# Later norm steps in TensorE's order, first FFN subtractions on VectorE, gated casts of weight sums, and w2's last units by halves, in a two-layer hybrid decoder

## The chip, the cores and the metric

The kernel runs on one core of a Trainium2 chip. The metric is device time in microseconds (us). TensorE is called PE below (its weight loads PEld), VectorE DVE, ScalarE ACT, GpSimd POOL, and SyncE SP. Each engine works through its own queue of instructions in order; an instruction waits until what it depends on has signalled.

## The reference

Two post-norm decoder layers over 528 tokens (16 meta tokens and 512 of the input), width 1024, FFN width 2816, all in float32. Cut to what matters:

```python
def hybrid_layer(h, ...):
    proj = jnp.einsum('bld,de->ble', h, w_in)
...
    mix = jnp.einsum('ble,ed->bld', mix, w_out)
    h = layer_norm(ALPHA * h + mix, ln1_g, ln1_b)
    a = jnp.einsum('bld,df->blf', h, w1)
    b = jnp.einsum('bld,df->blf', h, w3)
    y = jnp.einsum('blf,fd->bld', jax.nn.silu(a) * b, w2)
    return layer_norm(ALPHA * h + y, ln2_g, ln2_b)

def layer_norm(x, g, b):
    mu = jnp.mean(xf, axis=-1, keepdims=True)
    var = jnp.mean(jnp.square(xf - mu), axis=-1, keepdims=True)
    y = (xf - mu) * lax.rsqrt(var + LN_EPS)
    return (y * g + b).astype(x.dtype)
```

## The kernel before

**Layout.** Activations lie transposed: 128 of the 1024 channels on the partitions, the tokens along the row, so a full activation is eight tiles. The tokens are worked in two halves, A of 272 and B of 256 (A has 256 in the second layer's mixing and FFN, where the meta tokens are not needed any more). Every product is made of three matmuls on numbers split into a high and a low part: high by high, high by low, low by high (`mm3`, L237 to L239). So one output tile of a half (a unit) is 8 x 3 = 24 matmuls for a sum over 1024 channels, and 33 for one half of w2's 22 blocks.

**Weights** come in chunks of up to 1024 columns. `fetch` (L160) issues the chunk's DMA on SP into one of three `raw` buffers; `ensure` (L173) casts the high part on ACT (L183) and subtracts to get the low part (`sub_lo`, L140) on the engine that the chunk's entry names, DVE or POOL; there are four split buffers `w`. In the FFN the first three hidden blocks (`HEAD = 3`) go the plain way, the rest through a scheme of seven products with sums of weights and of activations (`fast`, L1069); for those, `sums_of` (L190) makes the sums of weights, tag S: a chunk's parts come by SP and by accumulating DMAs that POOL issues (L196, L197), ACT casts (L205, L208, L211, L214), DVE adds and subtracts. A gate (`tc.issue_after(marks["apply", e].ins)`) keeps those ACT and DVE instructions behind the latest marked instruction on their engine.

**The norms.** There are six, named by place and half: m0A and m0B behind layer 0's mixing, f0A and f0B behind its FFN, m1A and m1B behind layer 1's mixing. Each takes eight output tiles as they come: `evac` (L331) adds one to the residual, squares it (ACT L340, the last on DVE L338) and adds it to a running sum (L336) and a running sum of squares (L344), on DVE or POOL by a table; the last of these is `marks["sums"]`. Then three steps on PE. `stats(0)` transposes the sum in three or two blocks (L358), DVE reduces them (L359), and a matmul with ones (L362) spreads the mean. `stats(1)` transposes the sum of squares (L358), DVE reduces (L359) and forms the variance (L365 to L367), POOL takes the power -1/2 (L368), DVE puts it on a diagonal (L371). `apply` spreads that by a matmul (L375); DVE subtracts and multiplies each tile (L380, L381), ACT applies gain and bias (L311) and casts the high part (L313), POOL subtracts the low part (`xl`, L140). These `xh` and `xl` feed the next product. In the first layer POOL and DVE also rotate the retention's queries and keys (L581 to L590), with a DMA in between.

**The order of the work.** PE's instructions are written out by a planner (`Plan`, L60): a piece of work becomes due at the end of the pieces it depends on plus a lag from the table `LAG`, and pieces are issued in the order in which they become due by the planner's own clock. In LAG, `y`, `y2` and `st` are the lags before `stats(0)`, `stats(1)` and `apply`, with a suffix for the norm; `rs_1` is that of the retention output's state product in layer 1 (`ret_out`, L813, L819). A larger lag puts the step behind more of the other matmuls. The other engines' order is made by a scheduler from the same program.

**The FFN's first blocks** (`ffn_hidden`, L1155): three hidden blocks are made the plain way, w1's and w3's product each. ACT takes the silu of the w1 product (L1163). Meanwhile DVE and ACT make the sums of activations (`factors`, L1025: sums L1036 to L1040, high part Th by ACT L1042, low part Tl by DVE). The subtraction of chunks 0 to 3 goes to POOL where `CFG["n0"]` to `CFG["n3"]` is 1, otherwise to DVE; n2 and n3 are 1. On DVE these are placed behind `marks["sums"]`.

**w2 in layer 0** (`ffn_mid`, L1171): its 22 input blocks go in two rounds of 11. A unit's weights are two chunks, 1024 and 384 columns. In the second round units 0 to 5 run for A and B, unit 6 for A, 7 for A and B, then 6 for B from weights loaded again (L1218 to L1230).

Of the kernel before, what the change touches and what calls it, by code (L numbers as in the profile page):

```python
# [12 lines left out]
AF = mybir.ActivationFunctionType  # L13
# [16 lines left out]
EPS = 1e-5  # L30
# [2 lines left out]
N_IN = 21  # L33
PV_L = 40

LAG = dict(T=16.0, g2=3.0, y2=2.0, q=1.5, kb=4.25, fb=3.21, q_1=1.5, kb_1=5.0, fb_1=3.45, rot=8.62, vt=2.86, kt=3.84, kv=1.23, kvo=2.5, rs=2.5, ro=6.35, rp=0.69, f=12.8, a=5.62, b=0.77, v0=9.72, k=3.2, s=0.99, p=2.78, pt=1.24, mt=2.77, u=5.1, rm=3.74, pm=3.74, mx=3.25, y=0.8, st=2.25, ap=2.42, g=2.1, ga=8.46, gn=6.42, gt=21.89, gs=0.33, gs2=0.86, gl=2.0, w=10.8, rot_1=10.43, vt_1=1.2, kt_1=6.88, kv_1=0.74, kvo_1=1.6, rs_1=2.81, ro_1=7.28, rp_1=0.48, f_1=11.9, k_1=1.95, s_1=1.7, p_1=2.78, pt_1=1.16, mt_1=2.85, u_1=6.42, rm_1=3.0, pm_1=3.72, mx_1=3.17, y_m0A=0.8, y2_m0A=2.0, st_m0A=3.75, ap_m0A=2.42, y_m0B=1.6, y2_m0B=2.5, st_m0B=2.2, ap_m0B=2.42, y_f0A=0.8, y2_f0A=2.0, st_f0A=3.75, ap_f0A=2.42, y_f0B=1.6, y2_f0B=2.5, st_f0B=3.52, ap_f0B=2.42, y_m1A=0.8, y2_m1A=2.0, st_m1A=3.75, ap_m1A=2.42, y_m1B=1.6, y2_m1B=2.5, st_m1B=2.2, ap_m1B=3.15)

CFG = dict(h0=2, h1=1, h2=0, h3=2, h4=1, h5=2, h6=1, h7=2, g0=2, g1=1, g2=0, g3=0, g4=0, g5=2, g6=2, g7=1, p0=1, p1=0, p2=0, p3=0, p4=0, p5=0, p6=0, p7=0, q0=0, q1=1, q2=0, q3=1, q4=0, q5=1, q6=0, q7=1, pw=2, a3=7, a4=5, e1=7, e2=7, ws=1, wf=0, i0=2, i1=0, i2=0, i3=2, o0=1, o1=1, o2=0, o3=1, o4=1, o5=0, o6=1, o7=1, n0=0, n1=0, n2=1, n3=1, s1=1, s2=0, s3=0, s4=0, s5=1, s6=0, s7=0, t1=1, t2=0, t3=0, t4=1, t5=0, t6=0, t7=0)


def mix_half(c, qoff):
# [65 lines left out]
def hymba_kernel(ctx: ExitStack, tc: tile.TileContext, d: dict, out: bass.AP):  # L107
    nc = tc.nc
# [6 lines left out]
    rp = ctx.enter_context(tc.tile_pool(name="rp", bufs=3))  # L115
# [9 lines left out]
    marks = {}  # L125
# [43 lines left out]
    cut = 1024 - 256 * CFG["ws"]  # L169
# [49 lines left out]
    win_u, wout_u, w13_u, w2_u = [], [], [], []  # L219
    for l in range(DEPTH):  # L220
        win_u.append([add_chunks(d["w_in"][l, m], 1024, quarters if l == 0 and m < CFG["pw"] else (None, nc.gpsimd, nc.vector)[CFG[f"i{m}"]] if l and m < 4 else None)
                      for m in range(N_IN)])
        wout_u.append({h: [add_chunks(d["w_out"][l, m], 1024, nc.gpsimd if CFG[f"o{m}"] else nc.vector)
                           for m in range(KD)] for h in "AB"})
        w13_u.append([])
        for fs, cut in ((KH, slice(0, KH * P)), (KF, slice(KH * P, DFF))):
            for f in range(2 * KF)[len(w13_u[l]):2 * fs]:
                w13_u[l].append(add_chunks(d["w13"][l, f], 1024, f"S{1 + f % 2}" if f >= 2 * HEAD else
                                           nc.gpsimd if f < 4 and CFG[f"n{f}"] else nc.vector))
            if l < DEPTH - 1:  # L230
# [266 lines left out]
    def load_consts(l, ap_):  # L497
# [556 lines left out]
    def sums_of_x(n, hs, o, Th, Tl, units, ready):  # L1054
# [100 lines left out]
    def ffn_hidden(l, slot, put):  # L1155
        sa = {}

        def evac(key, half, ps):
            f, w = key
            n = ps.shape[-1]  # L1160
            if w == 0:
                s = sa[half, f] = slot(n)
                nc.scalar.activation(out=s, in_=ps, func=AF.Silu)  # L1163
            else:
                s = sa.pop((half, f))
                put(f, half, s, ps)

        us = list(zip(w13_u[l], [(f, w) for f in range(HEAD) for w in range(2)]))
        return us, evac

    def ffn_mid(l, x, ready, n_of, gp, hs, keep):  # L1171
        base = 16 + l * PV_L
        N = T // 2
        wf["pool"] = gp
        Th = gp.tile([P, 4, 3, N], F32R, name="Th")
# [36 lines left out]
        for i, fs in enumerate((range(KH), range(KH, KF))):
            if i:
                prev = plan.add(lambda: room(range(KH, KF)), 0.0, end, 9)
            last = fast(l, fs[0 if i else HEAD:], 0, N, Th, Tl, yslot, lambda f: (yslot(N), yslot(N)), gated, deps, prev)
            gdone.update({f: [(p, LAG["g2"])] for f, p in last.items()})
            end = [last[fs[-1]]]
            us = list(zip(w2_u[i], (*range(KD), KD - 2)))  # L1218
            for part, halves in ((us[:6], "AB"), (us[6:7], "A"), (us[7:8], "AB"), (us[8:], "B")) if i else ((us, "AB"),):
                dn.update(stage(part, lambda half, fs=fs: {f: tuple(g[:, :NA] if half == "A" else g[:, NA:] for g in gt[f]) for f in fs},  # L1220
                                list(fs), lambda h, key: n_of[h],
                                lambda m, half, ps, i=i: norm[half].evac(m, ps) if i else evac2(m, half, ps),
                                lambda half, key, k, end=end: gdone[k] + end, halves=halves, ahead=1 if i else 2, k0=fs[0]))
            end = [dn[us[-1][1], h] for h in "AB"]
        xn, nready = {}, {}
        for half in "AB":
            ap = norm[half].finish([dn[m, half] for m in (range(KD) if half == "A" else (0, 1, 2, 3, 4, 5, 7, 6))], base + 16, base + 24, xn)
            ap.append(plan.add(lambda half=half: free(keep[half]), 0.0, [ap[-1]], 0))
            for k in range(KD):
                nready[half, k] = (ap[-2], norm[half].lag["ap"] + 0.85 * k)  # L1230
        plan.run(ap)
        return xn, nready

    def ffn_last(l, x, ready, gp, hw, keep):
# [5 lines left out]
        def put(f, half, s, ps):  # L1240
# [283 lines left out]
```

## Time and profile before

| | |
|---|---|
| time, median of 3 runs (lowest to highest) | 1253.56 us (1252.38 to 1257.7) |
| profiled execution: its time, its span | 1256.85 us, 1254.7 us |
| mean granted clock of TensorE | 0.985 |
| busy: PE, DVE, ACT, POOL | 1194.9, 843.1, 602.5, 382.3 us |
| moved by DMA | 151.90 MB, mean 121 GB/s |

Views of the trace give times in us from the span's start. A timeline row is start, duration, engine, line, operation, output<-inputs, shapes, count, and in brackets the idle time before it with what ended it. In the view by stretches a row is the stretch, its length, PE's busy time with the number of groups, the granted clock, the share of the DMA engines and GB/s. Line numbers are those of the kernel before; the changed kernel has one line more near its top, so its L359 is the L358 of before.

### The profile page before, as it was taken

What the parts mean: (1) busy time and instruction counts of PE and PEld (TensorE: products, weight loads), DVE (VectorE), ACT (ScalarE), POOL (GpSimd) and SP (SyncE); (2) the same over time, 40 slices, a digit from 0 to 9 for tenths busy, and PEclk for the clock granted to TensorE, in tenths of its full rate; (3) what the DMA queues carried; (4) which work ended last, traced back from release to release, by engine and by line L of the source; (5) the groups of instructions that cost most, each with busy time, mean ns of one, the idle gap of its engine ahead of it and who ended that gap; (6) DMA issues with size and microseconds to landing.
All of it is one profiled execution on the core that took longest, in us unless ns stands there. A gap on an engine that the chain in (4) does not pass through costs nothing. (4 is left out here: it accounts for less than half of the span.)

```text
span 1254.7 us, 23592 instructions
## 1 busy us (share of the span) xinstructions
PE 1194.9 (95%) x9154; PEld 1143.2 (91%) x9154; DVE 843.1 (67%) x1724; ACT 602.5 (48%) x1178; POOL 382.3 (30%) x421
## 2 busy tenths in 40 slices
PE   7999999888999999999989999998779999999997
PEld 6989989888999999999989899998779999998885
DVE  6575686989785268864585756789857777762327
ACT  5435554555664146653264365455535555552222
POOL 5423447771110011101174243497411111100004
PEclk9999999989999999999989999999989999999998
DMA  6332212455763277732344221134547777633231
GB/s 234 105 106 68 69 34 68 144 152 143 170 162 99 93 185 180 181 81 77 103 128 126 79 78 64 35 118 154 149 116 185 174 188 175 157 106 101 86 101 68
DMA packets 58944, 151.90 MB, mean 121 GB/s; under 512 B 8328, under 2 KB 16808, under 8 KB 58832
## 3 DMA queue, kind: packets, MB, share of 16 engines
q1 hardware_dynamic: 47888, 130.46, 32.8%
q0 software_dynamic: 10944, 19.93, 9.8%
q8 instruction: 72, 1.18, 0.4%
q14 instruction: 40, 0.33, 0.1%
HBM read 144.38 MB, written 2.10 MB: 117 GB/s over the span
## 5 line engine op out<-in xcount | busy, mean ns | idle before, releaser
L237 PE MATMUL acc<-xh,w 128*128 128x256 f32 (+1 forms) x1024 | 303.2, 296 | 17.6 <-ACT y L1163 15.3
L238 PE MATMUL acc<-xl,w 128*128 128x256 f32 (+1 forms) x1024 | 295.2, 288 | 0.9 <-DVE xl L891 0.5
L239 PE MATMUL acc<-xh,w 128*128 128x256 f32 (+1 forms) x1024 | 294.4, 287 | 0.0
L140 DVE TENSOR_TENSOR w<-raw,w 128x1024 fp32r<-128x1024 f32 (+3 forms) x226 | 219.1, 989 | 69.9 <-ACT w L183 60.5
L183 ACT CAST w<-raw 128x1024 fp32r<-128x1024 f32 (+1 forms) x180 | 179.4, 997 | 160.2 <-PE acc L239 103.6
L237 PEld LDWEIGHTS acc<-xh,w 128*128 128x128 f32 x1024 | 197.8, 193 | 22.0 <-ACT y L1163 15.9
L238 PEld LDWEIGHTS acc<-xl,w 128*128 128x128 f32 x1024 | 198.0, 193 | 2.5 <-POOL xl L140 1.4
L239 PEld LDWEIGHTS acc<-xh,w 128*128 128x128 f32 x1024 | 197.6, 193 | 0.0
L140 POOL TENSOR_TENSOR w<-raw,w 128x256 fp32r<-128x256 f32 (+1 forms) x74 | 119.2, 1617 | 71.3 <-ACT w L183 63.2
L197 POOL DMA_DIRECT2D raw<-in_w x38 | 32.9, 865 | 353.9 <-DVE sr L209 83.8
L1140 PE MATMUL acc<-xh,w 128*128 128x264 f32 (+1 forms) x608 | 121.8, 283 | 0.0
L1140 PEld LDWEIGHTS acc<-xh,w 128*128 128x128 f32 x608 | 98.5, 188 | 0.2 <-ACT g L1098 0.2
L140 DVE TENSOR_TENSOR S<-sr,S 128x512 fp32r<-128x512 f32 x76 | 53.2, 702 | 54.1 <-ACT S L208 53.3
L1140 PE MATMUL acc<-xl,w 128*128 128x264 f32 (+1 forms) x304 | 85.4, 281 | 0.0
L298 POOL TENSOR_TENSOR r<-r,mhalf 128x1 f32<-128x1 f32 (+3 forms) x18 | 14.8, 821 | 186.3 <-DVE r L297 186.3
L1140 PE MATMUL acc<-Th,w 128*128 128x264 f32 (+1 forms) x304 | 61.3, 284 | 0.0
L1140 PE MATMUL one<-Th,S 128*128 128x264 f32 (+1 forms) x304 | 61.1, 283 | 0.0
L1140 PE MATMUL one<-xh,S 128*128 128x264 f32 (+1 forms) x304 | 60.9, 283 | 0.0
L1140 PE MATMUL acc<-Th,S 128*128 128x264 f32 (+1 forms) x304 | 60.9, 282 | 0.0
L1140 PE MATMUL one<-xh,w 128*128 128x264 f32 (+1 forms) x304 | 60.2, 282 | 0.0
L1140 PEld LDWEIGHTS acc<-xl,w 128*128 128x128 f32 x304 | 57.2, 188 | 0.0
L211 ACT CAST w<-raw 128x1024 fp32r<-128x1024 f32 x38 | 39.9, 1050 | 34.5 <-PE acc L1140 25.0
(492 smaller groups left out, 3134.1 us busy)
## 6 DMA issues: line engine op xcount, KB each, us to landing
raw<-in_w SPq DMA_DIRECT2D x88, 512.0 KB, 4.5
raw<-in_w_in SPq DMA_DIRECT2D x42, 512.0 KB, 3.8
raw<-in_w_out SPq DMA_DIRECT2D x32, 512.0 KB, 3.5
raw<-in_w2b SPq DMA_DIRECT2D x22, 512.0 KB, 3.4
s<-in_w SPq DMA_DIRECT2D x38, 256.0 KB, 4.6
s<-in_w POOLq DMA_DIRECT2D x38, 256.0 KB, 6.4
raw<-in_w POOLq DMA_DIRECT2D x38, 256.0 KB, 5.7
raw<-in_w2a SPq DMA_DIRECT2D x17, 512.0 KB, 3.6
```

Of the source, the lines that this page charges most:

```text
L140: return eng.tensor_tensor(lo, full, hi.bitcast(F32), op=ALU.subtract)
L183: nc.scalar.copy(w[:, 0, :n], raw[:, :n])
L197: nc.gpsimd.dma_start(a2[:, a], src1[:, a], accum_op=ALU.add)
L211: nc.scalar.copy(w2[:, 0], a2)
L237: nc.tensor.matmul(ps, lhsT=wh, rhs=hi, start=first, stop=False)
L238: nc.tensor.matmul(ps, lhsT=wh, rhs=lo, start=False, stop=False)
L239: nc.tensor.matmul(ps, lhsT=wl, rhs=hi, start=False, stop=last)
L298: nc.gpsimd.tensor_tensor(r[:np_, :nb], r[:np_, :nb], mhalf[:np_, :nb], op=ALU.pow)
L1140: nc.tensor.matmul(ps, lhsT=a[:, w], rhs=b, start=fresh and k == 0 and q == 0, stop=k == 3 and q == 2, skip_group_check=True)
```

## The change

```diff
+M2 = (0, 1, 2, 3, 4, 5, 6, 7, 6, 5, 4)
...
-LAG = dict(..., rs_1=2.81, ..., y2_m0A=2.0, st_m0A=3.75, ..., y_f0B=1.6, y2_f0B=2.5, ..., y2_m1A=2.0, st_m1A=3.75, ...)
+LAG = dict(..., rs_1=4.5, ..., y2_m0A=4.1, st_m0A=5.7, ..., y_f0B=2.5, y2_f0B=3.5, ..., y2_m1A=4.2, st_m1A=5.5, ...)
-CFG = dict(..., n2=1, n3=1, ...)
+CFG = dict(..., n2=0, n3=0, ...)
...
-                w2_u.append([add_chunks(d["w2a"][m][:, cut], KH * P, nc.vector) for m in (*range(KD), KD - 2)[:8 + (fs == KF)]])
+                w2_u.append([add_chunks(d["w2a"][m][:, cut], KH * P, nc.vector) for m in M2[:KD if fs < KF else None]])
...
-                nc.scalar.activation(out=s, in_=ps, func=AF.Silu)
+                marks["apply", "s"] = nc.scalar.activation(out=s, in_=ps, func=AF.Silu)
...
-            us = list(zip(w2_u[i], (*range(KD), KD - 2)))
-            for part, halves in ((us[:6], "AB"), (us[6:7], "A"), (us[7:8], "AB"), (us[8:], "B")) if i else ((us, "AB"),):
+            us = list(zip(w2_u[i], M2))
+            for part, halves in ((us[:4], "AB"), (us[4:7], "A"), (us[7:8], "AB"), (us[8:], "B")) if i else ((us, "AB"),):
...
-            ap = norm[half].finish([dn[m, half] for m in (range(KD) if half == "A" else (0, 1, 2, 3, 4, 5, 7, 6))], base + 16, base + 24, xn)
+            ap = norm[half].finish([dn[m, half] for m in (range(KD) if half == "A" else M2[:4] + M2[7:])], base + 16, base + 24, xn)
```

**Lags.** In PE's order m0A's second transpose stands 18 matmuls later and its L375 another 18 (54 matmuls between the two, 36 before); m1A's second transpose 24 later, with 54 matmuls to L375. L819 in layer 1 stands 12 or 24 matmuls later. On f0B see w2. The order around m0B and m1B on PE is as before.

**n2 and n3.** In both layers the low parts of the FFN's chunks 2 and 3 are made on DVE, behind the norm's last sum, and no longer on POOL. DVE at the end of m0B's sums, before (`y` are the sums, `w` the weights, `lnmv` the moments, `r` the reciprocal root):

```order
L336 TENSOR_TENSOR y<-y 128x256
L338 TENSOR_TENSOR y<-y 128x256
L344 TENSOR_TENSOR y<-y 128x256
L359 TENSOR_REDUCE lnmv<-one 128x2
L365 SCALAR_TENSOR_TENSOR r<-lnmv 128x2
L359 TENSOR_REDUCE lnmv<-one 128x2
L366 TENSOR_TENSOR r<-lnmv,r 128x2
L367 TENSOR_SCALAR r<-r 128x2
L371 TENSOR_SCALAR y<-c_ident,r 128x128 x2
```

and in the changed kernel:

```order
L337 TENSOR_TENSOR y<-y 128x256
L339 TENSOR_TENSOR y<-y 128x256
L345 TENSOR_TENSOR y<-y 128x256 x2
L141 TENSOR_TENSOR w<-raw,w 128x1024 x2
L360 TENSOR_REDUCE lnmv<-one 128x2 x2
L366 SCALAR_TENSOR_TENSOR r<-lnmv 128x2
L367 TENSOR_TENSOR r<-lnmv,r 128x2
L368 TENSOR_SCALAR r<-r 128x2
L372 TENSOR_SCALAR y<-c_ident,r 128x128 x2
```

Two subtractions of 128x1024 have come between the last sum and the first reduction; the two reductions now stand together.

**The mark.** `marks["apply", "s"]`, until now the last cast of a norm, is also each head silu, so ACT's casts of the weight sums that are made afterwards come behind it. ACT in layer 1's first FFN blocks, before (S are the weight sums, Th the sums of activations, L1163 the silu):

```order
L205 CAST S<-s_11231 128x512
L208 CAST S<-sr 128x512
L214 CAST S_11239<-sr 128x512
L205 CAST S<-s_11366 128x512
L183 CAST w<-raw 128x1024
L1163 ACTIVATE y<-acc 128x256
L183 CAST w<-raw 128x1024
L1042 CAST Th<-y 128x256
L214 CAST S_11374<-sr 128x512
```

and in the changed kernel (L1164 is the silu, L206, L209, L212 and L215 the four casts):

```order
L184 CAST w<-raw 128x1024
L1043 CAST Th<-y 128x256 x4
L1164 ACTIVATE y<-acc 128x256
L1043 CAST Th<-y 128x256 x2
L1164 ACTIVATE y<-acc 128x256 x2
L206 CAST S<-s_11251 128x512
L209 CAST S<-sr 128x512
L212 CAST w<-raw 128x1024
L215 CAST S_11259<-sr 128x512
```

The casts have moved behind the last of the head's silus.

**M2.** In the second round of w2 in layer 0, units 0 to 3 run for A and B, units 4, 5 and 6 for A, 7 for A and B, then 6, 5 and 4 for B from weights loaded again: two units more are loaded (four DMAs, four ACT casts and four DVE subtractions more), and the number of matmuls stays. Behind A's last unit stand 132 matmuls of B instead of 66, and behind those 24 matmuls of layer 1's first unit for A ahead of f0B's first transpose. POOL at this place, before (`xl` are the norm's low parts, 272 columns for A and 256 for B, L368 is f0B's power, L588 a multiply of the rotation that waits for a DMA):

```order
L140 TENSOR_TENSOR xl<-y,xh 128x272 x2
L634 AFFINE_SELECT mask<-mask 128x128
L140 TENSOR_TENSOR xl<-y,xh 128x272 x4
L368 TENSOR_TENSOR r<-r,mhalf 128x2
L140 TENSOR_TENSOR xl<-y,xh 128x272 x2
L140 TENSOR_TENSOR xl<-y,xh 128x256 x4
L588 TENSOR_TENSOR y<-y,rcs 128x272
L140 TENSOR_TENSOR xl<-y,xh 128x256 x4
```

and in the changed kernel (L369 the power, L589 the multiply):

```order
L141 TENSOR_TENSOR xl<-y,xh 128x272
L635 AFFINE_SELECT mask<-mask 128x128
L141 TENSOR_TENSOR xl<-y,xh 128x272 x2
L589 TENSOR_TENSOR y<-y,rcs 128x272
L369 TENSOR_TENSOR r<-r,mhalf 128x2
L141 TENSOR_TENSOR xl<-y,xh 128x256 x8
L141 TENSOR_TENSOR w<-raw,w 128x256 x2
L589 TENSOR_TENSOR y<-y,rcs 128x256
```

The multiply has moved ahead of f0B's power, and all eight `xl` of B behind both.

More of the change, by code (lines that the diff above doesn't have):

```diff
@@ L34 @@
 PV_L = 40
-LAG = dict(T=16.0, g2=3.0, y2=2.0, q=1.5, kb=4.25, fb=3.21, q_1=1.5, kb_1=5.0, fb_1=3.45, rot=8.62, vt=2.86, kt=3.84, kv=1.23, kvo=2.5, rs=2.5, ro=6.35, rp=0.69, f=12.8, a=5.62, b=0.77, v0=9.72, k=3.2, s=0.99, p=2.78, pt=1.24, mt=2.77, u=5.1, rm=3.74, pm=3.74, mx=3.25, y=0.8, st=2.25, ap=2.42, g=2.1, ga=8.46, gn=6.42, gt=21.89, gs=0.33, gs2=0.86, gl=2.0, w=10.8, rot_1=10.43, vt_1=1.2, kt_1=6.88, kv_1=0.74, kvo_1=1.6, rs_1=2.81, ro_1=7.28, rp_1=0.48, f_1=11.9, k_1=1.95, s_1=1.7, p_1=2.78, pt_1=1.16, mt_1=2.85, u_1=6.42, rm_1=3.0, pm_1=3.72, mx_1=3.17, y_m0A=0.8, y2_m0A=2.0, st_m0A=3.75, ap_m0A=2.42, y_m0B=1.6, y2_m0B=2.5, st_m0B=2.2, ap_m0B=2.42, y_f0A=0.8, y2_f0A=2.0, st_f0A=3.75, ap_f0A=2.42, y_f0B=1.6, y2_f0B=2.5, st_f0B=3.52, ap_f0B=2.42, y_m1A=0.8, y2_m1A=2.0, st_m1A=3.75, ap_m1A=2.42, y_m1B=1.6, y2_m1B=2.5, st_m1B=2.2, ap_m1B=3.15)
@@ L38 @@
-CFG = dict(h0=2, h1=1, h2=0, h3=2, h4=1, h5=2, h6=1, h7=2, g0=2, g1=1, g2=0, g3=0, g4=0, g5=2, g6=2, g7=1, p0=1, p1=0, p2=0, p3=0, p4=0, p5=0, p6=0, p7=0, q0=0, q1=1, q2=0, q3=1, q4=0, q5=1, q6=0, q7=1, pw=2, a3=7, a4=5, e1=7, e2=7, ws=1, wf=0, i0=2, i1=0, i2=0, i3=2, o0=1, o1=1, o2=0, o3=1, o4=1, o5=0, o6=1, o7=1, n0=0, n1=0, n2=1, n3=1, s1=1, s2=0, s3=0, s4=0, s5=1, s6=0, s7=0, t1=1, t2=0, t3=0, t4=1, t5=0, t6=0, t7=0)
+LAG = dict(T=16.0, g2=3.0, y2=2.0, q=1.5, kb=4.25, fb=3.21, q_1=1.5, kb_1=5.0, fb_1=3.45, rot=8.62, vt=2.86, kt=3.84, kv=1.23, kvo=2.5, rs=2.5, ro=6.35, rp=0.69, f=12.8, a=5.62, b=0.77, v0=9.72, k=3.2, s=0.99, p=2.78, pt=1.24, mt=2.77, u=5.1, rm=3.74, pm=3.74, mx=3.25, y=0.8, st=2.25, ap=2.42, g=2.1, ga=8.46, gn=6.42, gt=21.89, gs=0.33, gs2=0.86, gl=2.0, w=10.8, rot_1=10.43, vt_1=1.2, kt_1=6.88, kv_1=0.74, kvo_1=1.6, rs_1=4.5, ro_1=7.28, rp_1=0.48, f_1=11.9, k_1=1.95, s_1=1.7, p_1=2.78, pt_1=1.16, mt_1=2.85, u_1=6.42, rm_1=3.0, pm_1=3.72, mx_1=3.17, y_m0A=0.8, y2_m0A=4.1, st_m0A=5.7, ap_m0A=2.42, y_m0B=1.6, y2_m0B=2.5, st_m0B=2.2, ap_m0B=2.42, y_f0A=0.8, y2_f0A=2.0, st_f0A=3.75, ap_f0A=2.42, y_f0B=2.5, y2_f0B=3.5, st_f0B=3.52, ap_f0B=2.42, y_m1A=0.8, y2_m1A=4.2, st_m1A=5.5, ap_m1A=2.42, y_m1B=1.6, y2_m1B=2.5, st_m1B=2.2, ap_m1B=3.15)
@@ L41, in mix_half @@
+CFG = dict(h0=2, h1=1, h2=0, h3=2, h4=1, h5=2, h6=1, h7=2, g0=2, g1=1, g2=0, g3=0, g4=0, g5=2, g6=2, g7=1, p0=1, p1=0, p2=0, p3=0, p4=0, p5=0, p6=0, p7=0, q0=0, q1=1, q2=0, q3=1, q4=0, q5=1, q6=0, q7=1, pw=2, a3=7, a4=5, e1=7, e2=7, ws=1, wf=0, i0=2, i1=0, i2=0, i3=2, o0=1, o1=1, o2=0, o3=1, o4=1, o5=0, o6=1, o7=1, n0=0, n1=0, n2=0, n3=0, s1=1, s2=0, s3=0, s4=0, s5=1, s6=0, s7=0, t1=1, t2=0, t3=0, t4=1, t5=0, t6=0, t7=0)
 def mix_half(c, qoff):
```

## The prediction

> **What bounds the kernel now.** I read the page first, then the waits of TensorE (PE), its busy time by stretch, and its timeline at each wait. The page:
>
> ```profile
> PE 1194.9 (95%) x9154; PEld 1143.2 (91%) x9154; DVE 843.1 (67%) x1724; ACT 602.5 (48%) x1178; POOL 382.3 (30%) x421
> ...
> raw<-in_w2a SPq DMA_DIRECT2D x17, 512.0 KB, 3.6
> ```
>
> PE bounds it: 1194.9 us over 9154 matmuls, 0.13 us each. The change removes no matmul, so all it can win is PE's idle time, and time in which PE runs at a lower clock. The waits of PE say for whom it stops (columns: total, times, longest):
>
> ```profile
> PE acc L237 <- ACT y L1163: 15.3, 2, 10.6
> ...
> PE one L358 <- DVE y L336: 8.1, 3, 4.2
> PE one L358 <- DVE y L344: 5.5, 3, 2.0
> PE one L375 <- DVE y L371: 4.6, 3, 1.7
> PE one L819 <- DVE qx L807: 2.2, 2, 1.7
> ```
>
> All five stand where the diff reaches: the head silus (L1163), the norms' transposes (L358) and broadcast (L375), the retention output (L819). The stretches below give length, PE's busy time, matmuls in groups, and the granted clock; they are m0B, ffn0's head, f0, m1B and ffn1's head:
>
> ```profile
> 259.00:273.00 14.00, 10.33 (x57) 0.76 0.82 227
> 290.00:300.00 10.00, 5.29 (x30) 0.83 0.77 207
> 633.00:648.00 15.00, 10.67 (x55) 0.77 0.72 221
> ...
> 878.00:889.00 11.00, 6.77 (x41) 0.84 0.85 240
> 906.00:921.00 15.00, 4.43 (x26) 0.66 0.66 163
> ```
>
> I price what the clock costs as busy time x (1 - clock): 2.5, 0.9, 2.45, 1.1 and 1.5 us, 8.45 in all. PE's timeline gives each wait in its brackets, in the order m0A, m0B, ffn0, f0, m1A, m1B, ffn1:
>
> ```profile
> 235.08 0.55 PE L358 MATMUL one<-c_ident,y 128*128 128x128 f32 x3 [1.70 <-DVE y L344]
> ...
> 241.53 0.73 PE L375 MATMUL one<-y,ones 128*128 128x272 f32 x2 [1.71 <-DVE y L371]
> ...
> 263.33 0.41 PE L358 MATMUL one<-c_ident,y 128*128 128x128 f32 x2 [1.52 <-DVE y L336]
> ...
> 266.18 0.69 PE L358 MATMUL one<-c_ident,y 128*128 128x128 f32 x2 [2.01 <-DVE y L344]
> ...
> 295.66 0.52 PE L237 MATMUL acc<-xh,w 128*128 128x272 f32 x1 [4.71 <-ACT y L1163]
> ...
> 636.50 0.41 PE L358 MATMUL one<-c_ident,y 128*128 128x128 f32 x2 [2.33 <-DVE y L336]
> ...
> 647.51 0.67 PE L375 MATMUL one<-y,ones 128*128 128x256 f32 x2 [1.55 <-DVE y L371]
> ...
> 852.06 0.44 PE L358 MATMUL one<-c_ident,y 128*128 128x128 f32 x2 [1.83 <-DVE y L344]
> ...
> 858.13 0.70 PE L375 MATMUL one<-y,ones 128*128 128x256 f32 x2 [1.38 <-DVE y L371]
> ...
> 882.57 0.41 PE L358 MATMUL one<-c_ident,y 128*128 128x128 f32 x2 [4.23 <-DVE y L336]
> ...
> 917.17 0.58 PE L237 MATMUL acc<-xh,w 128*128 128x256 f32 x1 [10.57 <-ACT y L1163]
> ```
>
> With mix1's 1.7 (the longest for L807) these are 3.41 + 3.53 + 4.71 + 3.88 + 1.7 + 3.21 + 4.23 + 10.57 = 35.2 us. With the clock, 43.7 us are at stake.
>
> **The change part by part.** *m0A and m1A (y2, st).* m0A's second L358 goes 18 matmuls later, 18 x 0.13 = 2.3 us against its wait of 1.70; from there to L375 PE now has 54 matmuls where it had 36, 2.3 us more against 1.71. m1A's second L358 goes 24 later (3.1 against 1.83), and 54 matmuls (7.0 us) stand ahead of its L375, which came 858.13 - 852.06 = 6.1 us behind the transpose with its wait. Every wait has cover, by as little as 0.6 us. What PE does meanwhile is the next products of w_out, which need no norm. Gains 3.3 and 3.2; bounds 2 and 3.4, since VectorE (DVE) can be late by a step.
>
> *m0B and m1B (n2, n3).* The order of PE is unchanged here. DVE and GpSimd (POOL) side by side:
>
> ```profile
> 259.66 1.00 DVE L344 TENSOR_TENSOR y<-y 128x256 f32<-128x256 f32 x1
> ...
> 261.02 2.16 DVE L336 TENSOR_TENSOR y<-y 128x256 f32<-128x256 f32 x1
> 263.10 2.56 DVE L338 TENSOR_TENSOR y<-y 128x256 f32<-128x256 f32 x1
> 265.70 0.42 DVE L344 TENSOR_TENSOR y<-y 128x256 f32<-128x256 f32 x1
> ...
> 268.57 0.48 DVE L371 TENSOR_SCALAR y<-c_ident,r 128x128 f32<-128x128 f32 x2 [0.84 <-POOL r L368]
> ...
> 876.56 2.60 DVE L336 TENSOR_TENSOR y<-y 128x256 f32<-128x256 f32 x1 [1.00 <-POOL y L336]
> 879.08 2.56 DVE L344 TENSOR_TENSOR y<-y 128x256 f32<-128x256 f32 x1
> ...
> 288.90 1.21 DVE L140 TENSOR_TENSOR w<-raw,w 128x1024 fp32r<-128x1024 f32 x1
> ```
>
> ```profile
> 259.42 0.96 POOL L140 TENSOR_TENSOR xl<-y,xh 128x272 fp32r<-128x272 f32 x1
> 260.34 5.04 POOL L140 TENSOR_TENSOR w<-raw,w 128x1024 fp32r<-128x1024 f32 x2
> ...
> 876.47 4.88 POOL L140 TENSOR_TENSOR w<-raw,w 128x1024 fp32r<-128x1024 f32 x2
> ...
> 882.96 0.87 POOL L196 DMA_DIRECT2D s<-in_w  x1 [0.74 <-DMA s<-in_w]
> ```
>
> A sum that takes 0.42 alone takes 2.16 to 2.60 while POOL does the pair. Without the pair DVE is (2.16 - 0.42) + (2.56 - 0.42) = 3.9 us earlier at m0B and 4.3 at m1B: more than the 3.53 and 4.23 that PE waits. But the two subtractions now stand on DVE between the last sum and the first L359, 2 x 1.21 = 2.4 us; behind them wait L365 to L371, POOL's L368, and PE's L375. From the end of the last sum (266.12) to that of L371 (269.05) are 2.9 us, so 5.3 with them; PE has 24 matmuls there, 3.1 us, and y2 puts its second transpose 2.5 us behind the last product, 0.8 later than four DVE operations of 0.42 need for the sums. I take a new wait at L375 of 5.3 - 3.1 - 0.8 = 1.4 at m0B; at m1B one us more, for POOL's L196 that waits for a landing ahead of L368: 2.4. The clock: m0A's and m1A's single waits of 1.7 cost none, the pair 1.52 + 2.01 did, so a wait of 1.4 or 2.4 leaves it full. Gains 3.53 + 2.5 - 1.4 = 4.6 and 4.23 + 1.1 - 2.4 = 2.9; upper bounds 6.0 and 5.3.
>
> The lower bounds come from what stays on POOL, its xl: the L344 at 259.66 took 1.00 beside the xl that ended at 260.38, 0.58 more than alone. If each of four sums of a norm meets one, 4 x 0.58 = 2.3 us go: bounds 2.3 and 0.6. I take none of it, for the order doesn't say which sums meet an xl. The Trainium skill (SBUF — State Buffer, SBUF: two separate sides) says of the port pair that both engines share that whichever starts first has it for its whole instruction and "the other fully blocks"; by that page alone every meeting costs DVE the rest of the xl, and the total would be 1234. The row agrees: L344 ended 0.28 after the xl.
>
> *ffn1's head (the gate of the casts).* ScalarE (ACT) stands in a queue here:
>
> ```profile
> 294.91 0.41 ACT L1042 CAST Th<-y 128x264 fp32r<-128x264 f32 x1 [2.53 <-DVE y L1040]
> ...
> 635.96 1.05 ACT L183 CAST w<-raw 128x1024 fp32r<-128x1024 f32 x1
> ...
> 914.88 1.04 ACT L211 CAST w<-raw 128x1024 fp32r<-128x1024 f32 x1 [7.06 <-DMA raw<-in_w]
> ```
>
> L211 waited 7.06 us for a transfer that POOL accumulates, and the silu that PE needed stood behind it. Now the four casts of each weight sum come behind the last head silu. Of 10.57 us, 3.5 remain, since the silu still follows Th casts that DVE feeds; I take 4.0, as DVE also waits for the queue of subtractions. The clock stays low behind a 4 us wait (m1B's 4.23 cost 1.1): 1.3. Gain 10.57 + 1.5 - 4.0 - 1.3 = 6.8; bounds 4 to 12. The casts themselves then are late, but 48 head matmuls (6.3 us) stand between the silu and the first product that uses a sum.
>
> *ffn0's head* has the same gate and another cause: the silu stood behind a Th cast that waited 2.53 for DVE, and DVE is as full as before. The gate moves some DVE work of the sums behind the silu; I take 3.4 of the 4.71 as left, and 0.6 of the clock's 0.9: 1.6. POOL's raw accumulation (L197) now stands ahead of half B's xl and waits for its own landing: I charge 1.0. Gain 0.6; bounds -2 to 5.6.
>
> *f0 (M2, y, y2).* Two more single-half units of w2 are loaded: 4 more DMAs on SP, 4 casts on ACT (2 x 1.05 and two short ones), 4 subtractions on DVE (2 x 1.21 and two short), over eight half-units of 33 matmuls, 34 us: hidden while a unit's chunks come in time. Half A's norm then has 132 matmuls of half B as cover (17 us) instead of 66, and 24 A matmuls stand ahead of B's first transpose (3.1 against 2.33). Against it: that first A unit wants all eight x parts of A at once. ACT owes eight affines, eight casts of x and the chunks' casts in that cover, and POOL's memsets stand among the xl; I put the last xl about 3 us late. And on POOL the rotary multiply L588 now stands ahead of B's L368:
>
> ```profile
> 654.23 1.04 POOL L588 TENSOR_TENSOR y<-y,rcs 128x272 f32<-128x272 f32 x1 [0.67 <-DMA y<-y]
> ```
>
> It waits for a DMA, and L368, L371 and PE's L375 wait behind it; I put 2 us there against the 1.55 now. Of 3.88 + 2.45 = 6.3 some 5.0 stay. Gain 1.3; bounds -4 to 6.3, the least certain term.
>
> *mix1 (rs_1).* L819 goes 12 to 24 matmuls later, 1.6 to 3.1 us against 1.7: 1.5, bounds 0 to 2.2.
>
> The sum: 3.3 + 4.6 + 0.6 + 1.3 + 1.5 + 3.2 + 2.9 + 6.8 = 24.2 us. The profiled run took 1256.85 (span 1254.7), so 1232.6 in its terms; the median of the runs is 1253.56, 3.3 lower, with the same work in it, and I take the sum off the median: 1229.4.
>
> The Trainium skill (TensorE: Matmul & The Clock Gate, Part 1: The HAM clock gate) has the half clock come after an idle window of about 3.4 us and last about as long; by that page's figures the waits left at ffn0 and ffn1 would cost 1.7 each and not 0.6 and 1.3, an estimate of 1231. The trace differs in one place: at m0B a pair of waits of 1.52 and 2.01 was enough.
>
> **The rivals.** *All of it goes:* every wait finds cover, as at m0A. For it: no matmul is added. Against: DVE, at 67%, is the releaser of nearly all, and gets work here. 1253.56 - 43.7 = 1210.
>
> *The waits move on:* PE stops at the next step in order, L375 where it was L358, and the low ends meet: m0A 2, m1A 2, m0B 2.3, m1B 0.6, ffn0 -1, f0 -4, mix1 0, ffn1 6.8: 8.7, so 1244.9. For it: in m0B and m1B the chain behind the last sum grows by 2.4. Against: ffn1's wait has a single cause that goes.
>
> *The silu gate does not do what it says,* since the Th casts that DVE feeds hold the silu as long; with the former rival 1253.56 - 8.7 + 6.8 = 1251.7, no change that can be told.
>
> *Slower, by w2's supply in f0.* Six single-half units (33 matmuls, 4.3 us each) want two chunks each, through three raw buffers: three chunks in 6.4 us. A buffer's round is 3.6 (landing) + 1.05 + 1.21 = 5.9, so 0.5 us is spare. Each us above it costs 12 / 3 = 4 us over twelve chunks. To be 0.5% slower than now it must eat 24.2 + 6.3 us, so landing must rise by 0.5 + 7.6 to 11.7 us: then 1260. For it: the spare is thin. Against: 3.6 is the median, and PE shows no wait for w2 now.
>
> **How the numbers follow.** A measurement of this kernel tells about 0.5% (6.3 us) from no change. The forecast (within some 8 us of 1229) 0.56; all goes 0.13; the waits move on 0.21; no gain that shows 0.06; slower 0.04. Faster is 0.56 + 0.13 + 0.21 = 0.90, same 0.06, slower 0.04. The range reaches into both neighbours, to 1213 (of the gain of 43.7 all but 3) and to 1242, and leaves out about 2 in 10.
>
> **What would show it.** Right: PE's waits for L1163 at ffn1 fall from 10.6 to about 4; no L358 waits over 1 at m0A, m1A; DVE's sums at m0B and m1B fall to 0.4 to 1.0, with a wait of 1 to 2.5 at L375 behind them; clock 1.00 in m0B's stretch. Wrong: a new PE wait over 3 us at L375 of m0B or m1B, at w2's units (L237 for a cast of w), or in f0 for POOL's xl; or ffn1's silu still 8 us late.

## The result, and the profile after

The changed kernel takes 1247.19 us (median of 8 runs, 1244.89 to 1249.13), the kernel before 1254.05 (8 runs): ratio 0.994, 95% interval 0.9924 to 0.9955. That is 6.9 us faster, where 24.2 were forecast with a range down to 1213 and up to 1242. The sign was right, the size was not: the time lies 5 us above the upper end of the range.

The page of the changed kernel, then the waits of PE, sorted by total:

```profile
PE 1193.6 (96%) x9154; PEld 1142.3 (92%) x9154; DVE 844.5 (68%) x1732; ACT 603.7 (49%) x1182; POOL 374.9 (30%) x417
```

```profile
PE one L376 <- DVE y L372: 9.8, 4, 3.4
...
PE acc L238 <- DVE ka L141: 5.0, 3, 2.6
PE acc L239 <- POOL xl L141: 4.7, 3, 2.2
PE acc L238 <- ACT y L1164: 3.9, 2, 2.5
PE acc L238 <- DVE y L1186: 2.5, 1, 2.5
...
PE one L359 <- DVE y L345: 1.4, 2, 1.2
```

The waits for the silu fell from 15.3 to 3.9 and those at the transposes (L359, before L358) from 13.6 to 1.4. But L376 (before L375) rose from 4.6 to 9.8, and four waits are new or larger: those for ka (2.2 before), for xl (0.5), for the gating product L1186 (none) and, in a line left out here, for p at L738 (0.5 before, 2.1 now). The stretches of m0B, ffn0, f0, m1B and ffn1 in the changed kernel (length, PE's busy time, groups, granted clock, DMA share, GB/s):

```profile
255.00:269.00 14.00, 11.73 (x90) 1.00 0.81 237
284.00:298.00 14.00, 12.58 (x105) 1.00 0.49 132
628.00:643.00 15.00, 10.26 (x56) 0.77 0.72 233
874.00:887.00 13.00, 10.23 (x82) 1.00 0.81 231
898.00:912.00 14.00, 11.51 (x83) 0.88 0.59 150
```

The clock is full at m0B, ffn0 and m1B now; f0 is as it was.

Both kernels have 9154 matmuls, and their order differs only near the norms, at L819 and in w2's second round. So I compared the start of the matmul with the same number at the borders of the places; the difference between two borders is what a place gained (us, minus is a loss). The first row lies ahead of anything that the change touches. The kernels of the experiments gained 0.4 to 3.0 us in it against the profiled run of before, whatever they change: that run was slow there, 3.3 us above the first median, and it is no gain of the change. The other rows are read to about 1 us for the same reason; each column is one execution, and behind waits of the same length the clock can differ by 1.4 us of time (last section).

| place | predicted | changed kernel | e1 gate | e2 n2, n3 | e3 norm lags | e4 rs_1 | e5 w2 order |
|---|---|---|---|---|---|---|---|
| before m0A | 0 | 3.2 | 3.0 | 2.4 | 2.7 | 1.2 | 2.9 |
| m0A | 3.3 | -2.3 | 0.0 | 0.0 | -2.1 | 0.0 | 0.0 |
| m0B | 4.6 | -0.7 | 1.2 | 0.9 | -1.6 | 1.0 | 1.0 |
| ffn0 | 0.6 | 4.8 | 4.1 | 0.2 | 1.9 | -1.2 | -1.2 |
| f0 | 1.3 | -0.2 | -0.1 | 0.1 | -1.0 | 0.3 | -1.1 |
| mix1 | 1.5 | -3.4 | 1.0 | 0.9 | 1.2 | -2.5 | 0.0 |
| m1A | 3.2 | -1.9 | 0.0 | 0.0 | -1.2 | 0.0 | 0.0 |
| m1B | 2.9 | 2.9 | -0.1 | 0.9 | -3.7 | 0.2 | 0.0 |
| ffn1 | 6.8 | 8.0 | 9.5 | -1.1 | -0.5 | -1.7 | 0.1 |

One mark gives most of the gain, at ffn0 and ffn1 (e1, below); m1B's goes with n2 and n3 (e6 and e8); m0A, m1A and mix1, which the lags were to relieve, lost 7.6 us.

**m0A, where the first term failed.** DVE, POOL and PE in the changed kernel:

```profile
237.95 1.23 DVE L141 TENSOR_TENSOR w<-raw,w 128x1024 fp32r<-128x1024 f32 x1 [1.47 <-ACT w L184]
239.09 3.24 DVE L372 TENSOR_SCALAR y<-c_ident,r 128x16 f32<-128x16 f32 x3
```

```profile
236.24 0.86 POOL L369 TENSOR_TENSOR r<-r,mhalf 128x3 f32<-128x3 f32 x1 [0.97 <-DVE r L368]
...
238.31 1.45 POOL L345 TENSOR_TENSOR y<-y 128x256 f32<-128x256 f32 x1 [0.49 <-ACT y L341]
239.72 2.33 POOL L141 TENSOR_TENSOR w<-raw,w 128x1024 fp32r<-128x1024 f32 x1
```

```profile
242.39 0.87 PE L376 MATMUL one<-y,ones 128*128 128x272 f32 x2 [3.37 <-DVE y L372]
```

L372 needs POOL's power, done at 237.10. It starts at 239.09, because a weight subtraction that waits for its cast stands ahead of it on DVE, and then takes 3.24 beside POOL. In the kernel before, L371 stood ahead of that subtraction on DVE, though it was long there too:

```profile
238.75 2.72 DVE L371 TENSOR_SCALAR y<-c_ident,r 128x16 f32<-128x16 f32 x3 [0.98 <-POOL r L368]
...
243.81 1.28 DVE L140 TENSOR_TENSOR w<-raw,w 128x1024 fp32r<-128x1024 f32 x1
```

The lag y2 moved the whole of `stats(1)` later in the program, its DVE steps with it, and the next weight chunk came in front. The two waits of 1.70 and 1.71 became one of 3.37, and the clock dropped behind it (last section). m1A reads the same, with 2.78.

**mix1.** Moving L819 did two things. First, 12 matmuls of `mm3` now stand ahead of it (L820 in the changed kernel), and they need an accumulator that DVE's subtractions for ka free. PE, whose order is written out, waits for them (DVE, then PE):

```profile
697.54 0.89 DVE L141 TENSOR_TENSOR ka<-acc,ka 64x256 fp32r<-64x256 f32 x2
```

```profile
698.11 0.36 PE L238 MATMUL acc<-xh,w 128*128 128x256 f32 x1 [2.59 <-DVE ka L141]
```

Second, what hangs on L819 moved as well:

```profile
701.33 0.76 DVE L830 BATCH_NORM_STATS2 gst<-one 128x6 f32<-128x96 f32 x4 [2.01 <-PE one L824]
...
705.18 0.16 DVE L835 SCALAR_TENSOR_TENSOR nb<-gmv,r 128x4 f32<-128x4 f32 x1 [1.13 <-POOL r L299]
705.37 0.42 DVE L141 TENSOR_TENSOR ka<-acc,ka 64x256 fp32r<-64x256 f32 x1
...
708.31 0.89 DVE L141 TENSOR_TENSOR ka<-acc,ka 64x256 fp32r<-64x256 f32 x2
```

```profile
708.88 0.36 PE L238 MATMUL acc<-xh,w 128*128 128x256 f32 x1 [1.62 <-DVE ka L141]
```

The retention's group statistics now wait for PE on DVE. The subtraction for ka at 705.37, whose cast was done at 704.63, waits behind them, and so does the one at 708.31, which frees the accumulator that PE waits for.

**Behind m0B** stands a row that nothing in the prediction had, DVE and POOL:

```profile
273.02 5.67 DVE L207 TENSOR_TENSOR sr<-s,raw 128x512 f32<-128x512 f32 x1
...
279.33 0.43 DVE L1186 TENSOR_TENSOR y<-y,acc 128x272 f32<-128x272 f32 x1
```

```profile
272.29 5.84 POOL L141 TENSOR_TENSOR xl<-y,xh 128x256 fp32r<-128x256 f32 x8
```

The same addition took 1.00 in the kernel before (at 277.98). Here it ends 0.56 us after the eighth xl, and L1186 and PE (2.49) wait for it.

### The profile page after: what moved, and what is told of

The parts are those of the page before. It is cut to its first block, busy times and chain, and to the rows that moved or that the text cites. A ratio compares the mean times of both kernels' runs of the same rounds, so it can differ in the third digit from the quotient of the medians.

```text
span 1244.8 us, 23626 instructions
## 1 busy us (share of the span) xinstructions
PE 1193.6 (96%) x9154; PEld 1142.3 (92%) x9154; DVE 844.5 (68%) x1732; ACT 603.7 (49%) x1182; POOL 374.9 (30%) x417
## 5 line engine op out<-in xcount | busy, mean ns | idle before, releaser
L141 DVE TENSOR_TENSOR w<-raw,w 128x1024 fp32r<-128x1024 f32 (+3 forms) x234 | 225.7, 984 | 67.4 <-ACT w L184 63.5
L184 ACT CAST w<-raw 128x1024 fp32r<-128x1024 f32 (+1 forms) x184 | 182.5, 993 | 163.1 <-PE acc L240 104.0
L141 POOL TENSOR_TENSOR w<-raw,w 128x256 fp32r<-128x256 f32 (+1 forms) x70 | 111.3, 1595 | 76.4 <-ACT w L184 70.1
L198 POOL DMA_DIRECT2D raw<-in_w x38 | 32.8, 864 | 329.0 <-DMA raw<-in_w 102.9
L197 POOL DMA_DIRECT2D s<-in_w x38 | 37.8, 1002 | 61.5 <-DVE g L1243 12.3
```

The source lines that it names most:

```text
L141: return eng.tensor_tensor(lo, full, hi.bitcast(F32), op=ALU.subtract)
L184: nc.scalar.copy(w[:, 0, :n], raw[:, :n])
L197: nc.gpsimd.dma_start(r1, src2[:, b], accum_op=ALU.add)
L198: nc.gpsimd.dma_start(a2[:, a], src1[:, a], accum_op=ALU.add)
```

## The experiments

All are timed against the kernel before on the same chip; the base is named at each. The theory that I brought to them: the gate alone makes the gain, and the other edits move waits, since DVE's queue in order, and not PE's order, sets when the norms' steps are done. The rivals are the terms of the prediction.

**e1, the gate alone.**

```diff
-                nc.scalar.activation(out=s, in_=ps, func=AF.Silu)
+                marks["apply", "s"] = nc.scalar.activation(out=s, in_=ps, func=AF.Silu)
```

> The kernel before with the silu mark alone. Theory (the gate carries the gain at both FFN heads, and the other edits together cost some 5 us): ffn1's wait for L1163 falls from 10.6 to about 2.5 and ffn0's from 4.7 to about 1.5, 8.0 and 4 us of gain, so about 1242, faster than the changed kernel. Rival (ffn0's gain comes from n2 and n3, which free POOL): only ffn1's 8 us, about 1246, and ffn0's wait stays above 4.

Measured: 1240.28 us, ratio 0.9883 (0.9866 to 0.99), 15 us faster than before, and 7 us faster than the changed kernel. The rows of PE at ffn0 and ffn1:

```profile
288.83 0.39 PE L237 MATMUL acc<-xh,w 128*128 128x272 f32 x1 [2.13 <-ACT y L1163]
...
899.93 0.38 PE L237 MATMUL acc<-xh,w 128*128 128x256 f32 x1 [2.47 <-ACT y L1163]
```

ffn0's wait fell from 4.71 to 2.13 with n2 and n3 as they were. The rival falls: the gate carries both heads.

**e2, n2 and n3 alone.**

```diff
-CFG = dict(..., n2=1, n3=1, ...)
+CFG = dict(..., n2=0, n3=0, ...)
```

> The kernel before with n2 = n3 = 0 alone. Theory (the two subtractions on DVE put a new wait at L375 of some 2 us in m0B and m1B, and an addition of DVE gets locked out beside POOL's xl behind m0B): no more than 2 us of gain, 1252 to 1254. Rival (the prediction's term for m0B and m1B): 7.5 us of gain, 1246.5.

Measured: 1251.58, ratio 0.9974 (0.9964 to 0.9984), 3.7 us faster by the medians: between the two. The sums are 0.42 and the waits at L358 of m0B and m1B are gone, as predicted, but the new wait at L375 is larger (DVE, POOL and PE at m0B):

```profile
259.68 2.35 DVE L140 TENSOR_TENSOR w<-raw,w 128x1024 fp32r<-128x1024 f32 x2
...
266.80 0.48 DVE L371 TENSOR_SCALAR y<-c_ident,r 128x128 f32<-128x128 f32 x2 [3.63 <-POOL r L368]
```

```profile
264.02 2.00 POOL L196 DMA_DIRECT2D s<-in_w  x2 [6.12 <-DMA s<-in_w]
265.39 1.37 POOL L368 TENSOR_TENSOR r<-r,mhalf 128x2 f32<-128x2 f32 x1
```

```profile
267.33 0.70 PE L375 MATMUL one<-y,ones 128*128 128x256 f32 x2 [4.04 <-DVE y L371]
```

4.04 against the predicted 1.4, and 3.27 at m1B against 2.4. The 2.35 on DVE are as priced. Behind them L371 waits 3.63 for POOL, where it waited 0.84 before: POOL's L196 stand ahead of L368 and wait for a landing, at m0B too.

**e3, the lags of m0A and m1A alone.**

```diff
-LAG = dict(..., y2_m0A=2.0, st_m0A=3.75, ..., y2_m1A=2.0, st_m1A=3.75, ...)
+LAG = dict(..., y2_m0A=4.1, st_m0A=5.7, ..., y2_m1A=4.2, st_m1A=5.5, ...)
```

> The kernel before with the lags of m0A and m1A alone. Theory (L375 waits as long as L358 and L375 together did, since a weight subtraction has come ahead of L371 on DVE): between no change and 3 us slower, 1254 to 1257, with a wait of 2.8 to 3.4 at L375 in both places. Rival (the prediction's term): 6.5 us of gain, 1247.5, no wait over 1.

Measured: 1258.97, ratio 1.0029 (1.0017 to 1.0041), 3.7 us slower. L375 waits 3.34 at m0A, as in the changed kernel; at m1A it does not: the weight subtraction stands ahead of L371 there too, but L371 takes 0.96 (3.05 in the changed kernel). Instead PE waits 1.52 and 2.54 at L237 for DVE's L331. The largest loss lies one norm on, in m1B (DVE and POOL):

```profile
878.90 6.86 DVE L344 TENSOR_TENSOR y<-y 128x256 f32<-128x256 f32 x2
```

```profile
879.88 2.63 POOL L140 TENSOR_TENSOR w<-raw,w 128x1024 fp32r<-128x1024 f32 x1
882.18 1.00 POOL L140 TENSOR_TENSOR xl<-y,xh 128x256 fp32r<-128x256 f32 x1
882.86 2.61 POOL L140 TENSOR_TENSOR w<-raw,w 128x1024 fp32r<-128x1024 f32 x1
```

A later norm A leaves its xl on POOL among B's weight subtractions, and the second of these two sums of B comes out 0.29 us after POOL's last; the first took 0.42.

**e4, rs_1 alone** (`rs_1=2.81` to `rs_1=4.5`).

> The kernel before with rs_1 = 4.5 alone. Theory (L819 later makes the group statistics later on DVE, and the ka subtractions that PE needs stand behind them): 3.4 us slower, 1257.5, with waits of 1.6 to 2.6 of PE for ka. Rival (the prediction's term; what mix1 lost in the changed kernel comes from elsewhere): 1.5 us of gain, 1252.5.

Measured: 1257.92, ratio 1.0024 (1.0011 to 1.0036), 2.6 us slower: L819's wait is gone, and PE waits for ka 4.7 us in three places. The prediction's term has the wrong sign. The theory has the size, and its mechanism for the wait of 1.62, which stands behind the group statistics. The largest, 2.26, comes ahead of them: it is the 12 matmuls that now stand ahead of L819, as in the changed kernel.

**e5, w2's order and f0B's lags alone** (M2 and what uses it, `y_f0B=2.5, y2_f0B=3.5`).

> The kernel before with w2's new order and f0B's two lags alone. Theory (half A's last xl are late by as much as B's statistics were before, so f0's loss changes its place): no change, 1253 to 1257, PE waiting some 4 us for xl in f0 and no longer for L336. Rival (the sum of the other parts' own runs, -15.0, -3.7, +3.7 and +2.6, against the changed kernel's -8.1, leaves +4.3 for this part): about 1259.5.

Measured: 1255.93, ratio 1.0009 (1.0 to 1.0018): no change that can be told. L336's wait of 2.33 is gone; three waits for xl of 1.60, 2.19 and 0.92 have come in its place.

**e6, the gate with n2 = n3 = 0** (e1's and e2's edits).

> The gate and n2 = n3 = 0 together, without the new lags and w2's new order. Theory (the two parts act at different places): 15.0 + 3.7, about 1236.5. Rival (at ffn0 the two meet, the subtractions that DVE does before L359 delaying what the silu waits for): 1238 to 1241, no better than the gate alone.

Measured: 1238.43, ratio 0.9871 (0.9853 to 0.9888). The interval holds both figures; the median is the rival's, its reason is not. By the places it gained 2.3 at m0B and 1.5 at m1B against before, and 2.6 at ffn0 where the gate alone gained 4.1. But the wait for the silu there is 2.12, as with the gate (2.13); what differs is the granted clock behind it, 0.86 in place of 1.00 (last section).

**e7, the gate with the lag st alone**, so that PE does L375 later and DVE keeps its order.

```diff
-LAG = dict(..., st_m0A=3.75, ..., st_m1A=3.75, ...)
+LAG = dict(..., st_m0A=5.7, ..., st_m1A=5.5, ...)
```

> The gate, and of m0A's and m1A's lags only st (5.7 and 5.5), with y2 as it was. On DVE L371 then stands ahead of the weight subtraction again, and PE has 54 matmuls ahead of L375. Theory (y2 spoils the lags by putting that subtraction ahead of L371): PE's waits for L358 stay, 1.7 and 1.8, those at L375 of 1.7 and 1.4 go, some 3 us better than the gate alone, 1237. Rival (DVE is late for L375 whatever stands ahead, since POOL stretches L371): L375 waits again, no better than the gate alone, 1240 or more.

Measured: 1241.55, ratio 0.9897 (0.9882 to 0.9913), no better than the gate. Both were wrong in how. L375 waits no more at m0A and m1A, so y2 was what had spoilt it. But PE stops a few matmuls further on, here at m0A:

```profile
247.75 0.41 DVE L331 SCALAR_TENSOR_TENSOR y<-y,acc 128x256 f32<-128x256 f32 x1
```

```profile
248.30 0.36 PE L237 MATMUL acc<-mixBf,w 128*128 128x256 f32 x1 [2.45 <-DVE y L331]
```

L331 empties PE's accumulator for half B. It stands on DVE behind the subtractions and products of A's `apply`, which start later, since L375 is later. The wait moved a second time.

**e8, the gate with n2 = 0 and n3 = 1.**

> The gate and n2 = 0 alone: of the two subtractions one goes to DVE and one stays on POOL. Theory (the new wait at L375 comes from what stands ahead of L359 on DVE and from the weight sums' DMAs behind it): L375 waits 1.2 less than with both, L336 and L344 are stretched by one POOL subtraction at most; better than the gate alone by 3 to 6 us, 1234 to 1237. Rival (one subtraction on POOL still stretches a sum by 2.1 us, and DVE pays for the other): as the gate alone, 1240.

Measured: 1237.79, ratio 0.9859 (0.9843 to 0.9876), the fastest of those with the whole computation, 9.4 us less than the changed kernel by the medians. Against e1 it has one subtraction fewer on POOL; m0B is as with the gate and m1B 2.3 better. From e6 it can't be told by the intervals.

**e9, the work itself taken away.** Base e8; the low part of each w_out chunk is a copy by ACT in place of a subtraction.

```diff
     def sub_lo(eng, lo, full, hi):
+        if eng is nc.scalar:
+            return eng.copy(lo, full)
...
-        wout_u.append({h: [add_chunks(d["w_out"][l, m], 1024, nc.gpsimd if CFG[f"o{m}"] else nc.vector)
+        wout_u.append({h: [add_chunks(d["w_out"][l, m], 1024, nc.scalar)
```

> The gate and n2 = 0 (1237.8 us), and the low part of every w_out chunk is made by an ACT copy in place of a subtraction on DVE or POOL, so that the w_out product is not the reference's; that takes some 40 us of work off DVE and POOL in the stretches of m0A, m0B, m1A and m1B and puts 1.05 us a chunk on ACT. Lags as before. Theory (in these stretches PE waits because DVE and POOL are full and stretch each other, not because a step stands too early): the waits for L358 and L375 at m0A and m1A, 6.6 us together, go without any change of order, and with m0B's and m1B's sums unstretched about 10 us go: 1228. Rival (the chain of the statistics is too long for the matmuls in between, whatever DVE has to do): 1.5 us stay at each, 1234 or more.

Measured: 1233.31, ratio 0.9825 (0.9809 to 0.984). At m0A and m1A it gained 3.9 and 4.0 us: PE's four waits there are gone, with the lags of before. DVE and PE at m0A:

```profile
234.63 0.62 DVE L373 TENSOR_SCALAR y<-c_ident,r 128x16 f32<-128x16 f32 x3
```

```profile
236.70 0.62 PE L377 MATMUL one<-y,ones 128*128 128x272 f32 x2
```

L373 is L371 of before: 0.62 where it took 2.72, and no bracket on PE's row. So the chain fits between the matmuls as they were; DVE and POOL were too full for it. The time came 5 us short of the theory's, because L375 waits 3.9 at m0B and 2.5 at m1B, where it waited 0.9 and not at all in e8. The one subtraction that stays on POOL (n3's) now falls into the norm's own chain, here at m0B (DVE, then POOL):

```profile
259.54 3.23 DVE L369 TENSOR_SCALAR r<-r 128x2 f32<-128x2 f32 x1
```

```profile
260.08 2.65 POOL L142 TENSOR_TENSOR w<-raw,w 128x1024 fp32r<-128x1024 f32 x1
```

L369 is L367 of before, which takes 0.17 in e8.

**e10, e9 with the norm lags of e3.**

> As the last, with the lags y2 and st of m0A and m1A as in the change. Theory: with DVE and POOL relieved nothing stands ahead of L371 and L331 for long, and no wait for the norms over 0.5 us is left at m0A and m1A; the time is that of the last kernel, within 2 us. Rival (the later order costs by itself, since the norm's half A is ready later for the next product): 3 us slower than the last, as e3 was against before.

Measured: 1235.4, ratio 0.9838 (0.9814 to 0.9862), 2.1 us over e9 by the medians, and the intervals overlap: not settled. m0A and m1A gain 3.9 and 4.0 here too.

**e11 and e12, the clears.** Base e8, with w2's new order (e11) and without (e12); in both the clears of the mixing's buffers go from POOL to DVE.

```diff
-                nc.gpsimd.memset(t, 0.0)
+                nc.vector.memset(t, 0.0)
...
-            nc.gpsimd.memset(m, 0.0)
+            nc.vector.memset(m, 0.0)
```

> The gate and n2 = 0, w2's new order with f0B's lags, and the clearing of the mixing's buffers (states, mask and the small ones) on DVE and not on POOL. Theory (in f0 half A's xl are late on POOL, where the clears of 2.5 us stand between them): PE's 4.7 us for xl there fall to about 2, so some 2 us better than the gate and n2 = 0 alone, 1235.5. Rival (ACT's casts of xh are late themselves, or the clears stand in DVE's way as well): no gain, 1238 or more.

> The gate and n2 = 0, with the clears on DVE, w2 in the old order: the control of the last. Theory: f0's 2.3 us for L336 stay, since the sums of half B are late there and not the xl; as without it, 1237.8, within 1.5 us. Rival (POOL's clears are what makes f0 late in the old order as well): 3 us better, 1234.8.

Measured: e11 1238.67, ratio 0.9864 (0.9845 to 0.9883); e12 1242.66, 0.9904 (0.9883 to 0.9924). In e11 PE's waits for xl fell from 4.7 to 1.6 and f0 gained 1.9 against before (e8: 0.3); in the whole time nothing shows. In e12 f0 lost 1.8: the clears stand on DVE ahead of half B's sums, and L358 waits 5.3. So POOL's clears are a part of what made the new order of w2 worth nothing at f0, and moving them helped with that order alone.

## Why the prediction was wrong

The place named as bound was right: PE waits, and the waits lay where the rows showed them. The sum failed in these steps, the places that lost first (us of gain, predicted against measured in the changed kernel):

- **m0A and m1A, 6.5 against -4.2.** The step that failed: "Every wait has cover". The prediction counted the matmuls ahead of L375 and took the DVE chain to it as fixed. It isn't: y2 also moved the chain's place in DVE's queue, behind a weight subtraction, and the rows of L371 (2.72) that showed DVE and POOL full there went unread in the sum. e3 shows the lags alone to cost 3.7 us (2.1 and 1.2 of it at these two places), e7 that without y2 the wait moves on to L331, and e9 that the waits go when DVE and POOL are relieved.
- **m0B, 4.6 against -0.7.** The sums were freed and the clock is full, as the step said. Two sizes were off: the wait at L375 (2.04 in the changed kernel, 4.04 in e2, for 1.4), because L196's landing, charged to m1B alone, holds L368 at m0B as well; and the 5.67 us of L207, which cost PE 2.5 at L1186. The 5.67 goes with POOL's accumulating DMA (L198 after, L197 before), which holds the xl until a transfer has landed. Where it comes late, all eight xl are ready and run without a gap. In e12, without the new lags, it came at 271.49, and the addition took 5.54 and PE waited 2.5; in e1 at 269.23, POOL had gaps for ACT's casts, and the addition took 0.99. "I charge 1.0" for that DMA stood at ffn0; its price fell here, on DVE.
- **mix1, 1.5 against -3.4.** L819's wait went as said. But the matmuls put ahead of it were taken as ready, and 12 of them wait 2.59 for their accumulator; and what hangs on L819 on DVE was not followed (1.62 more). e4 shows the loss with that lag alone.
- **f0, 1.3 against -0.2.** The mechanism held: xl late, by 4.7 us in place of the estimated 3. L588 ahead of L368 cost little: no wait over 1 us stands at f0's L376 in the changed kernel.
- **ffn0, 0.6 against 4.8.** Mis-sized. The wait fell to 1.42 and not to 3.4, and the clock stayed full as well (1.00, it was 0.83), which is in part chance: with waits of 2.1 it was 1.00 in e1 and 0.86 in e6. "DVE is as full as before" was wrong: with its casts, the low parts of the weight sums leave the way to the silu. In the kernel before they took 3.6 us of DVE there, rows that the prediction had not read:

```profile
280.86 1.13 DVE L140 TENSOR_TENSOR S<-s,S 128x512 fp32r<-128x512 f32 x1 [0.39 <-ACT S L205]
281.91 1.83 DVE L140 TENSOR_TENSOR S<-sr,S 128x512 fp32r<-128x512 f32 x2
...
284.43 0.68 DVE L140 TENSOR_TENSOR S<-s,S 128x512 fp32r<-128x512 f32 x1
```

  In e1, where the gate gives 4.1 at this place, none of them stands ahead of the silu that PE waits for.
- **ffn1, 6.8 against 8.0**: right. The wait left is 2.46 for an expected 4.0.
- **m1B, 2.9 against 2.9**: right in the sum, not in its parts. L375 waits 1.58 for the predicted 2.4, and 1.19 is left at the transpose, since a sum meets an xl (the two sums at L345 take 2.21). The prediction had named such meetings for its lower bound and took none.

Of the rivals "the waits move on" was the one that came, at 0.21: its 1244.9 is 2.3 us off. Its mechanism (L375 where it was L358) is the first row of the waits after; that the number is so close is luck. By place it is off by up to 5.8 us (ffn0, -1 against 4.8; m0A, 2 against -2.3), and the errors cancel. What it missed is that a wait can also grow when it moves.

The parts add up: -15.0 (e1), -1.9 (e6 against e1), +3.7 (e3), +2.6 (e4) and +1.3 (e5) make -9.3 against the measured -6.9. The 2.4 us between them are not explained; the spread of six medians and the parts' acting on each other could both make them.

## What to carry to other kernels

When a step of one engine is put later in a written order, ask which instructions of other engines are issued with it, and what will then stand ahead of them in their queues; matmuls in between cover only a chain that keeps its place. Where a wait is released by an engine that is busy at that point, and whose short operations come out at five times their length, take work away from it first: here a later step on PE alone only moved the wait. And try each part of a change by itself: here one line was worth 15 us, and the rest gave half of it back.

## What the runs showed of the hardware

**DVE beside POOL.** An operation of DVE can be held through a whole run of POOL instructions. An addition that took 1.00 in the kernel before took 5.67 and ended 0.56 after the last of eight xl in a row. In e3 the second of the two sums at m1B, alone 0.42, took 6.41 (from 879.35) and ended 0.29 after the last of three POOL subtractions. In the first case DVE began 0.7 us after POOL's train. In the second it began 0.5 us ahead of POOL's first subtraction, while POOL was issuing a DMA (L196, from 879.20). So the price of a meeting is not one POOL instruction, as the prediction had it, but up to the whole train. The Trainium skill (SBUF — State Buffer, SBUF: two separate sides) has the pair of ports locked for one whole instruction; these rows agree with the blocking, and show it lasting over several. They don't agree with that page's words that whichever starts first has the pair: by the start times in the second case that was DVE, unless the issue of the DMA counts as POOL's start.

It is not always the whole train. In the kernel before, a sum at m0B came out 0.28 us after each of POOL's two subtractions (the prediction's rows at 260.34, 261.02 and 263.10). The records tell the two apart: in the trains that held DVE, each POOL instruction starts 0.28 to 0.35 us before the one ahead of it ends; in that pair it is 0.04. In all 14 profiles DVE's two-input operations of over 1.3 us were held past every overlap of the first kind and past none of 0.06 or less. Whether the overlap is the cause of the holding or comes with it is not shown.

**The clock.** A single wait of PE of 2.04 us (m0B in the changed kernel) left the granted clock at 1.00 in its stretch; the single waits at L376 of 3.37 (m0A) and 2.78 (m1A) in the changed kernel did not:

```profile
855.00:868.00 13.00, 10.22 (x62) 0.74 0.47 170
240.00:250.00 10.00, 7.61 (x49) 0.83 0.31 106
```

By the prediction's way of pricing it, busy time x (1 - clock), that is 2.7 and 1.3 us more than the waits themselves: why m0A and m1A lost time although their waits are no longer in all than before.

Between these, the length of the wait does not settle it. The wait at ffn0 is 2.13 in e1 and 2.12 in e6, that at ffn1 2.47 in e1 and 2.46 in the changed kernel. The stretches of e1 and e6 at ffn0, then e1 at ffn1:

```profile
284.00:294.00 10.00, 7.87 (x65) 1.00 0.49 134
284.00:296.00 12.00, 9.88 (x70) 0.86 0.53 151
893.00:908.00 15.00, 12.53 (x106) 1.00 0.54 141
```

In the changed kernel ffn1's stretch is at 0.88. Each drop costs 1.4 us by the same pricing. So the prediction's reading that a wait of 2.4 leaves the clock full was not safe; what decides between the two cases is not shown.
